# Nine pairs of z and gate tiles by seven block products, ahead of the state-space stage and through DRAM

## The chip, the cores and the metric

One core of a Trainium2 chip runs the whole decoder layer in a single launch. Its engines run side by side and meet at semaphores: TensorE (PE in the profile; its weight loads are PEld), VectorE (DVE), ScalarE (ACT) and GpSimd (POOL). SyncE (SP) and, for some tiles, ACT issue the DMAs. The metric is the device time of one execution in microseconds, the median of three runs.

## The reference, cut to what matters

The input is 1024 tokens of 1024 channels in float32. The first step multiplies them by one wide matrix; its columns are split into z, the state-space input xbc, dt, q, k, v and the gates:

```python
proj = jnp.einsum('bsd,dc->bsc', h, w_in[l])
z, xbc, dt_raw, q, k, v, gates = jnp.split(proj, SPLIT_POINTS, axis=-1)
y_ssm = mamba2_branch(z, xbc, dt_raw, ...)      # y * silu(z), then a norm over each group
y_attn = swa_sink_attention(q, k, v, ...)       # window of 128 keys, 16 heads
g_ssm, g_attn = jnp.split(jax.nn.sigmoid(gates + b_gate[l]), 2, axis=-1)
merged = (g_ssm * jnp.einsum('bsi,id->bsd', y_ssm, w_branch_ssm[l])
          + g_attn * jnp.einsum('bsi,id->bsd', y_attn, w_branch_attn[l]))
```

After the merge come an output projection, a layer norm, a feed-forward block with short convolutions, and a second layer norm. z and the gates have 2048 columns each, so 16 tiles of 128 columns each. z is used only after the state-space result of its channels exists; the gates are used only at the merge.

## The kernel before, in words

All large products run on PE with a split of every float32 factor into a high part (a cast on ACT) and a low part (the difference, on DVE or POOL); three products of parts (high by high, high by low, low by high) replace one. `dense(i)` makes one tile of 128 columns of the first projection: it loads and splits the weights (`load_w`, L103; the low part on POOL), and issues 8 x 3 x 2 = 48 matmuls of 512 moving columns into a PSUM tile `pd` of two banks. The pool `pd` has two buffers.

The program runs in stages:

- **Start.** x arrives transposed in 8 tiles and is split into `xh`, `xl`.
- **State-space stage.** Four groups of heads, `g` = 0 to 3. Each needs a B tile, a C tile and four xs tiles (`load_b`, `load_c`, `load_xs`: a dense tile, a convolution of three DVE operations out of PSUM, a silu). In each group `prep(g, hf)` and four times `unit(g, hf, i)` run for the first half of the sequence (`hf` = 0) and then for the second (`hf` = 1). Between the pieces of the first half and behind the second `prep`, `go()` places one of the six dense tiles of the next group (the gates 0 to 5 in the last group). In the second half each `unit(g, 1, i)` is followed by `zgate(g, i)`: a dense tile of z, a tanh, a DVE product out of PSUM, and the product with y.
- **Attention stage.** Tiles of k and v, then eight pairs of heads: a dense q tile, scores (`psc`), mask, bias and softmax over ACT, DVE and POOL, transposes (`ptp`), two masked copies on DVE, products with v (`py`). Gates 6 to 15 are dense tiles as well: `GPAT` places four of them behind the first halves of the first four pairs of heads, the others follow behind the pairs, and the last (`HOLD`) is issued behind the last `py`.
- **Branch projections** (`pbr`), **output projection** (`pmix`) with the first layer norm, **feed-forward** and **down projection** (`pdn`). The feed-forward block already makes its tiles two at a time with seven products of half size in place of eight (`prod`, `pair_s`, `head`, `mid`, `tail`): four half-size sums of weights, four of activations, 7 x 12 = 84 matmuls of 512 columns for two tiles.

The program is written in this order, and a scheduler then reorders the instructions of each engine by their place in the text and by when it takes their operands to be ready. Each engine runs its list in order. PSUM and SBUF tiles come from pools with a fixed number of buffers; a pool opened in the place of a closed one waits for its last readers. The tiles `tmp` of the pool `sp` have two buffers and serve the silu of xbc, the tanh of z and the first gates.

## Time and profile before

| | |
|---|---|
| median of 3 runs | 2023.79 us (2021.73 to 2023.85) |
| profiled execution | 2022.09 us, of which the instructions span 2020.3 us |
| PE busy | 1975.2 us, 98% of the span |
| DVE busy | 1351.0 us, 67% |
| POOL, ACT busy | 788.8 us (39%), 704.1 us (35%) |
| DMA | 197.5 MB moved, 98 GB/s on average |

Matmuls overlap in the pipeline, so "busy" of PE adds up durations that lie on top of each other: one matmul of 512 columns is on record with 394 ns, but the next one starts 0.227 us after it. What PE can do in a stretch is therefore read from starts, not from mean durations.

### The profile page before, as it was taken

To read this page: it belongs to the slowest core of one execution; us is meant where nothing else is said; L and a number is where in the kernel's file an instruction comes from. 1 tells how busy PE (TensorE), PEld (TensorE's weight loads), DVE (VectorE), ACT (ScalarE), POOL (GpSimd) and SP (SyncE) were. 2 spreads that over 40 slices of the span, in tenths; PEclk is the share of its full clock that TensorE was granted. 3 is DMA by queue.
4 is the path that set the end of the run, shared out by engine and by line. 5 is a ranking of instruction groups with operands and counts; after the bars stand their busy time and mean duration, and the time that the engine had idled before them with its cause. 6 is when DMAs were issued, how large, how long until landed. Compare 5 with 4: busy or idle time off the path is not lost.

```text
span 2020.3 us, 24472 instructions
## 1 busy us (share of the span) xinstructions
PE 1975.2 (98%) x9780; PEld 1614.6 (80%) x9780; DVE 1351.0 (67%) x1669; ACT 704.1 (35%) x921; POOL 788.8 (39%) x449
## 2 busy tenths in 40 slices
PE   8999999999999999999999998989999999999997
PEld 5888888888888788888888886867788888878886
DVE  6668576776355367874355368877889988863367
ACT  3334333333233334433311234234444444432122
POOL 2233233223231244442000045349999999500023
PEclk9999999999999999999999998999999999999999
DMA  4213312222332312114333344112221221264221
GB/s 161 78 60 102 126 55 94 87 81 77 112 115 84 94 53 74 42 74 157 104 105 134 137 156 156 53 55 74 92 94 73 84 94 73 81 234 154 83 84 63
DMA packets 82578, 197.50 MB, mean 98 GB/s; under 512 B 6496, under 2 KB 33696, under 8 KB 82464
## 3 DMA queue, kind: packets, MB, share of 16 engines
q1 hardware_dynamic: 76944, 191.14, 27.0%
q10 hardware_dynamic: 5520, 4.79, 0.9%
q8 instruction: 77, 1.26, 0.2%
q14 instruction: 37, 0.30, 0.0%
HBM read 153.82 MB, written 42.09 MB: 97 GB/s over the span
## 4 chain that ended last, share of the span: by engine, by line
PE 70%; issue 14%; DVE 7%; POOL 4%; DMA 3%; ACT 1%; SPq 0%; DVEq 0%; ACTq 0%; POOLq 0%
PE pd L183 32%; PE pdn L1017 11%; PE pb L724 6%; PE pc L724 4%; PE pa L724 4%; PE pmix L822 3%; PE yd L354 2%; PE yo L346 2%; PE psc L501 1%; PE py L541 1%; PE pst L320 1%; POOL sl L101 1%; DMA raw<-in_wup 1%; PE px L311 1%; DMA bsc<-trow 1%
## 5 line engine op out<-in xcount | busy, mean ns | idle before, releaser
L183 PE MATMUL pd<-xl,whi_in 128*128 128x512 f32 x1056 | 336.0, 394 | 0.0
L183 PE MATMUL pd<-xh,wlo_in 128*128 128x512 f32 x1056 | 333.8, 393 | 0.0
L183 PE MATMUL pd<-xh,whi_in 128*128 128x512 f32 x1056 | 332.8, 394 | 0.2 <-DVE xs L128 0.2
L101 POOL TENSOR_TENSOR wlo_in<-wraw_in,whi_in 128x1024 fp32r<-128x1024 f32 x66 | 162.4, 2461 | 366.6 <-ACT whi_in L100 353.1
L183 PEld LDWEIGHTS pd<-xh,whi_in 128*128 128x128 f32 x1056 | 197.2, 188 | 44.0 <-issue 3.4
L183 PEld LDWEIGHTS pd<-xl,whi_in 128*128 128x128 f32 x1056 | 197.2, 188 | 42.8 <-issue 3.8
L183 PEld LDWEIGHTS pd<-xh,wlo_in 128*128 128x128 f32 x1056 | 197.2, 188 | 40.2 <-issue 1.5
L101 POOL TENSOR_TENSOR sl<-S,sh 128x512 fp32r<-128x512 f32 x88 | 161.3, 1844 | 3.7 <-ACT sh L100 3.7
L100 ACT CAST whi_in<-wraw_in 128x1024 fp32r<-128x1024 f32 x66 | 69.4, 1051 | 209.7 <-PE pd L183 128.1
L684 POOL TENSOR_TENSOR ba<-ba,bs 128x1024 f32<-128x1024 f32 x7 | 18.8, 2694 | 259.3 <-DVE ba L683 259.3
L660 PE MATMUL pbr<-yl,whi_br 128*128 128x512 f32 x384 | 117.8, 389 | 0.0
L660 PE MATMUL pbr<-yh,wlo_br 128*128 128x512 f32 x384 | 117.4, 389 | 0.0
L660 PE MATMUL pbr<-yh,whi_br 128*128 128x512 f32 x384 | 116.7, 389 | 0.0
L1017 PE MATMUL pdn<-dh,ah 128*128 128x512 f32 x352 | 110.1, 390 | 0.6 <-ACT ah L100 0.6
L1017 PE MATMUL pdn<-dh,al 128*128 128x512 f32 x352 | 109.8, 390 | 0.3 <-DVE al L101 0.3
L1017 PE MATMUL pdn<-dl,ah 128*128 128x512 f32 x352 | 109.7, 389 | 0.0
L128 DVE SCALAR_TENSOR_TENSOR cs<-cg,colt,cs 128x1023 f32<-128x1023 f32 (+1 forms) x44 | 101.1, 2298 | 5.1 <-ACT cs L126 4.6
L583 POOL TENSOR_TENSOR out<-out,lnt 128x512 f32<-128x512 f32 x16 | 20.2, 1284 | 200.3 <-ACT out L582 200.3
L100 ACT CAST sh<-S 128x512 fp32r<-128x512 f32 x88 | 53.9, 621 | 105.2 <-POOL S L759 83.5
L128 DVE SCALAR_TENSOR_TENSOR cs<-cv,colt,cs 128x1023 f32<-128x1023 f32 (+1 forms) x44 | 85.4, 1940 | 2.0 <-ACT cs L126 2.0
L660 PEld LDWEIGHTS pbr<-yh,whi_br 128*128 128x128 f32 x384 | 72.1, 188 | 15.0
L660 PEld LDWEIGHTS pbr<-yh,wlo_br 128*128 128x128 f32 x384 | 72.1, 188 | 15.0
(305 smaller groups left out, 4321.9 us busy)
## 6 DMA issues: line engine op xcount, KB each, us to landing
wraw_in<-in_win SPq DMA_DIRECT2D x66, 512.0 KB, 3.5
m<-acd SPq DMA_DIRECT2D x32, 512.0 KB, 4.5
yraw<-ysc SPq DMA_DIRECT2D x24, 512.0 KB, 4.7
wraw_br<-in_wbr SPq DMA_DIRECT2D x24, 512.0 KB, 3.5
uraw<-in_wup SPq DMA_DIRECT2D x22, 512.0 KB, 3.5
raw<-in_wup SPq DMA_DIRECT2D x22, 512.0 KB, 4.2
asc<-cs SPq DMA_DIRECT2D x22, 512.0 KB, 2.6
draw<-in_wdn SPq DMA_DIRECT2D x22, 512.0 KB, 3.5
```

The lines of the kernel that those rows point to most:

```text
L100: A.copy(hi, raw)
L101: (eng or V).tensor_tensor(lo, raw, f(hi), ALU.subtract)
L128: V.scalar_tensor_tensor(h[:, s:], p[:, :T - s], col(c0 + taps - 1 - s), h[:, s:], ALU.mult, ALU.add)
L183: PE.matmul(p[:, q * 512:(q + 1) * 512], w[:, k * P:(k + 1) * P], x[:, q * 512:(q + 1) * 512], start=k == 0 and n == 0, stop=k == KT - 1 a ...
L311: PE.transpose(px[:, i * P:(i + 1) * P], txs[g, i][:, c * P:(c + 1) * P], ident)
L320: PE.matmul(pst, bn[:, j * P:(j + 1) * P], xdd, start=True, stop=True)
L346: PE.matmul(yo[:, j * P:(j + 1) * P], sts[j][:, i * P:(i + 1) * P], tcc[g][:, c * P:(c + 1) * P], start=True, stop=True)
L354: PE.matmul(yd[hh * 64:hh * 64 + 64, j * P:(j + 1) * P], xdts[j][:, i * P + hh * 64:i * P + hh * 64 + 64], m[:, hh, j * P:(j + 1) * P], st ...
L660: PE.matmul(p[:, q * 512:(q + 1) * 512], w[:, o:o + P], x[:, q * 512:(q + 1) * 512], start=k == 0 and n == 0, stop=k == 3 and n == 2)
L724: PE.matmul(p, a[w][:, k * P:(k + 1) * P], bop[b][x][:, k, :], start=onto is None and k == 0 and n == 0, stop=k == 3 and n == 2, skip_grou ...
L822: PE.matmul(p[q], x[tq][:, k, ts_], w[:, q * 512:(q + 1) * 512], start=k == 0 and n == 0, stop=k == KT - 1 and n == 2)
L1017: PE.matmul(p[q], x[:, j], w[:, q * 512:(q + 1) * 512], start=j == 0 and n == 0, stop=j == nf - 1 and n == 2)
```

## The change

Eighteen dense tiles leave their places: twelve of z (i = 0, 1, 2 of each group) and the gates 8 to 13. They are made in nine pairs, in a stage of their own between the start and the state-space stage, each pair by seven half-size products: 7 x 12 = 84 matmuls in place of 96. For it four sums of x are made while x arrives (on DVE, then split), and four sums of weights for each pair (on DVE, for the first pair on POOL). The results, with the tanh applied, are written to DRAM; `zgate` reads z back into a `tmp` tile, and the merge reads the gates from DRAM as it did. The gates 6 and 7 are made as ordinary dense tiles while x arrives, before the B and C tiles. Only z tiles i = 3 stay dense in the state-space stage, and only the gates 14 and 15 stay in the attention stage; the list behind `GPAT` runs out after the second pair of heads, and no gate is left for the place behind the last `py`.

```diff
+GATES = list(range(G3, 16))
+SZ = [4 * g + i for g in range(4) for i in range(3)]
+SG = GATES[2:8]
...
+        XO = [0, 4, 1, 5, 2, 6, 3, 7]
...
+            if n % 2:
+
+                p_, q_ = rawk[k - 4], raw
+                lo_, hi_ = slice(0, 512), slice(512, 1024)
+                V.tensor_tensor(p_[:, lo_], p_[:, hi_], p_[:, lo_], ALU.subtract)
+                V.tensor_tensor(p_[:, hi_], q_[:, hi_], p_[:, hi_], ALU.subtract)
+                V.tensor_tensor(q_[:, hi_], q_[:, hi_], p_[:, lo_], ALU.subtract)
+                V.tensor_tensor(q_[:, lo_], q_[:, lo_], q_[:, hi_], ALU.subtract)
+                split(q_, tb_[0][:, k - 4], tb_[1][:, k - 4])
+                split(p_, ta[0][:, k - 4], ta[1][:, k - 4])
...
+            def out0(kind, i, r):
+
+                if kind == "z":
+                    t = oo.tile([P, T], F32, tag="zt", bufs=1, name="zt")
+                    A.activation(t, r, AF.Tanh, scale=0.5)
+                    V.scalar_tensor_tensor(r, t, 1.0, r, ALU.add, ALU.mult)
+                    nc.sync.dma_start(zsc[i], r)
+                else:
+                    A.activation(r, r, AF.Tanh, bias=col(C_GB + i), scale=0.5)
+                    nc.sync.dma_start(gsc[i], r)
...
+            for i in GATES[:2]:
+                cc[i] = dense(TG + i, XO)
...
+            def prod0(p, a, b, first):
+                for k in range(4):
+                    for n, (w, x) in enumerate(((0, 0), (0, 1), (1, 0))):
+                        PE.matmul(p, a[w][:, k * P:(k + 1) * P], bop0[b][x][k],
+                                  start=first and k == 0 and n == 0, stop=k == 3 and n == 2,
+                                  skip_group_check=not first)
...
+                E = G if j == 0 else V
+                sr = {v: so.tile([P, 512], F32, tag=f"S{v}", bufs=1, name=f"S{v}") for v in range(1, 5)}
+                E.tensor_tensor(sr[1], raw1[:, lo_], raw1[:, hi_], ALU.add)
+                E.tensor_tensor(sr[2], sr[1], raw[:, lo_], ALU.subtract)
+                E.tensor_tensor(sr[3], raw[:, lo_], raw1[:, lo_], ALU.subtract)
+                E.tensor_tensor(sr[4], raw[:, hi_], sr[2], ALU.subtract)
+                for v, src in ((2, sr[2]), (1, sr[1]), (3, sr[3]), (5, raw1[:, hi_]), (4, sr[4])):
+                    t = "a22" if v == 5 else "s"
+                    h, l = (so.tile([P, 512], F32R, tag=t + w, bufs=2 if v == 5 else 4, name=t + w) for w in "hl")
+                    split(src, h, l, E)
...
+            for j in range(len(todo)):
+                head0(j)
+                if j + 1 < len(todo):
+                    if j + 1 not in R:
+                        first0(j + 1)
+                if j:
+                    tail0(j - 1)
+                mid0(j)
+                if j + 1 < len(todo):
+                    sums0(j + 1)
+            tail0(len(todo) - 1)
...
-                pz = dense(TZ + 4 * g + i)
                 t = sp.tile([P, T], F32, tag="tmp", name="tz")
-                A.activation(t, pz, AF.Tanh, scale=0.5)
-                V.scalar_tensor_tensor(t, t, 1.0, pz, ALU.add, ALU.mult)
+                if 4 * g + i in zsc:
+                    nc.sync.dma_start(t, zsc[4 * g + i])
+                else:
+                    pz = dense(TZ + 4 * g + i)
+                    A.activation(t, pz, AF.Tanh, scale=0.5)
+                    V.scalar_tensor_tensor(t, t, 1.0, pz, ALU.add, ALU.mult)
                 V.tensor_tensor(x, x, t, ALU.mult)
...
-            gates = list(range(15, G3 - 1, -1))
+            gates = [i for i in range(15, G3 - 1, -1) if i not in GATES[:2] + SG]
...
-                    for _ in range(GPAT[2 * hp + hf]):
+                    for _ in range(GPAT[2 * hp + hf] if gates else 0):
```

The scheduler's lists show what this does to the order. The first place is PE in the second half of group 2 (units 0 to 2; `yo` and `yd` are a unit's products, `pd` the dense tiles, `xh`, `xl` the parts of x). Before:

```order
L346 MATMUL yo<-cT_1836,st_5_3190 128x128
L346 MATMUL yo<-cT_1836,st_6_3204 128x128
L354 MATMUL yd<-m,xdt 64x128 x6
L183 MATMUL pd_3499<-xl_186,whi_in_3495 128x512
L183 MATMUL pd_3499<-xh_185,wlo_in_3496 128x512 x2
L183 MATMUL pd_3499<-xh_195,whi_in_3495 128x512 x2
L183 MATMUL pd_3499<-xl_196,whi_in_3495 128x512 x2
L183 MATMUL pd_3499<-xh_195,wlo_in_3496 128x512
L346 MATMUL yo<-cT_1836,st_7_3218 128x128
```

Now, at the same units:

```order
L513 MATMUL yo<-cT_3129,st_4_3868 128x128
L513 MATMUL yo<-cT_3129,st_5_4315 128x128
L513 MATMUL yo<-cT_3129,st_6_4329 128x128
L521 MATMUL yd<-m,xdt 64x128 x6
L513 MATMUL yo<-cT_3129,st_7_4343 128x128
L513 MATMUL yo<-cT_3129,st_4_3868 128x128
L513 MATMUL yo<-cT_3129,st_5_4315 128x128
L513 MATMUL yo<-cT_3129,st_6_4329 128x128
L513 MATMUL yo<-cT_3129,st_7_4343 128x128
L521 MATMUL yd<-m,xdt 64x128 x10
```

The dense tile that stood between the units' products is gone; in the list of the change, 46 rows in a row, from the `yd` of unit 2 of the first half to the `yo` of the last unit of the second, hold no matmul of a dense tile.

The second place is PE at the end of the attention stage. Before, the last pairs of heads:

```order
L183 MATMUL pd_7220<-xl_206,whi_in_7216 128x512
L541 MATMUL py<-pcur,vn 64x128
L183 MATMUL pd_7220<-xl_206,whi_in_7216 128x512
L526 MATMUL ptp<-idt,s_6928 128x128 x4
L183 MATMUL pd_7220<-xh_205,wlo_in_7217 128x512 x2
L183 MATMUL pd_7220<-xh_215,whi_in_7216 128x512 x2
L183 MATMUL pd_7220<-xl_216,whi_in_7216 128x512 x2
L183 MATMUL pd_7220<-xh_215,wlo_in_7217 128x512 x2
L541 MATMUL py<-pcur,vn 64x128
```

Now:

```order
L711 MATMUL py<-pprv,vn 64x128 x2
L696 MATMUL ptp<-idt,s_7476 128x128 x4
L711 MATMUL py<-pcur,vn 64x128
L696 MATMUL ptp<-idt,s_7513 128x128 x4
L711 MATMUL py<-pcur,vn 64x128 x3
L711 MATMUL py<-pprv,vn 64x128 x2
```

From the last matmul of the last q tile to the first `pbr` the list of the change holds 96 `psc`, 64 `ptp` and 135 `py`, and no dense tile; from the first `psc` to there it holds 403 dense matmuls, where the list before has 783.

The third place is SP's list in the second half of group 1, where the reads of z (`tz`) are new, ahead of loads that stood there already (`m` for a unit, `wraw_in` for a dense tile):

```order
L531 DMA tz<-zsc_118 128x1024
L500 DMA m<-acd 128x2x512
L531 DMA tz<-zsc_119 128x1024
L111 DMA wraw_in_4139<-in_win 128x1024
L500 DMA m<-acd 128x2x512 x2
L111 DMA wraw_in_4228<-in_win 128x1024
```

A `tz` row waits for one of the two `tmp` buffers, and the rows behind it wait with it.

## Rows read from the trace of the kernel before

**Rows 1.** The page, part 1: busy time of each engine, share, instructions.

```profile
PE 1975.2 (98%) x9780; PEld 1614.6 (80%) x9780; DVE 1351.0 (67%) x1669; ACT 704.1 (35%) x921; POOL 788.8 (39%) x449
```

**Rows 2.** The chain in order of time: start us, length us, what, count.

```profile
86.92 10.91 PE pd L183 x48
...
1506.55 2.72 PE pc L724 x12
...
1525.59 2.72 PE pc L724 x12
```

**Rows 3.** Windows: length, busy us by engine (count), PEclk granted, DMA, GB/s.

```profile
346.50:487.20 140.70, 140.70 (x761) 114.61 (x760) 100.09 (x118) 50.44 (x57) 43.42 (x24) 1.00 0.23 82
...
689.40:942.80 253.40, 252.79 (x1600) 208.35 (x1600) 176.38 (x352) 99.20 (x199) 104.95 (x80) 1.00 0.19 66
...
1470.00:1650.00 180.00, 180.00 (x795) 148.90 (x794) 164.19 (x115) 80.42 (x105) 168.31 (x85) 1.00 0.23 85
```

**Rows 4.** Windows: attention up to the first pbr, and a later stretch.

```profile
689.40:953.70 264.30, 263.69 (x1647) 217.37 (x1648) 181.21 (x356) 102.79 (x204) 104.95 (x80) 1.00 0.22 77
1200.00:1250.00 50.00, 42.16 (x169) 33.44 (x168) 41.34 (x44) 20.68 (x26) 28.14 (x11) 0.90 0.52 186
```

**Rows 5.** DVE groups, 346.5 to 487.2 us: busy us, mean ns | idle before.

```profile
L343 DVE TENSOR_TENSOR m<-m,cbm 128x1024 f32<-128x1024 f32 x8 | 11.2, 1406 | 0.1
L340 DVE TENSOR_TENSOR m<-m,acn 128x1024 f32<-128x1024 f32 x8 | 10.6, 1322 | 0.5 <-ACT ee L337 0.5
L350 DVE SCALAR_TENSOR_TENSOR ee<-xs,colt,ee 128x512 f32<-128x512 f32 x8 | 8.1, 1014 | 0.0
L366 DVE TENSOR_TENSOR xs<-xs,tz 128x1024 f32<-128x1024 f32 x5 | 6.7, 1346 | 0.1
...
L349 DVE TENSOR_TENSOR ee<-yo,ee 128x512 f32<-128x512 f32 x8 | 5.5, 685 | 2.9 <-PE yo L346 2.9
...
L128 DVE SCALAR_TENSOR_TENSOR xs<-pd,colt,xs 128x1022 f32<-128x1022 f32 x4 | 5.1, 1276 | 0.1
L365 DVE SCALAR_TENSOR_TENSOR tz<-tz,pd 128x1024 f32<-128x1024 f32 x4 | 4.9, 1218 | 2.5 <-ACT tz L364 2.5
```

**Rows 6.** DVE groups of the attention stage, 689.4 to 942.8 us.

```profile
L513 DVE TENSOR_TENSOR s<-s,bias 128x512 f32<-128x512 f32 x32 | 23.7, 742 | 0.3
L530 DVE TENSOR_TENSOR pcur<-ptp,cstt 128x512 f32<-128x512 f32 x32 | 21.9, 686 | 21.1 <-PE ptp L526 20.7
...
L520 DVE TENSOR_REDUCE mx<-s 128x4 f32<-128x512 f32 x32 | 21.9, 683 | 38.7 <-ACT s L518 38.5
...
L511 DVE COPY_PREDICATED s<-cstt,psc 128x256 f32<-128x256 int32 x48 | 20.2, 440 | 4.0 <-ACT s L510 3.9
...
L486 DVE SCALAR_TENSOR_TENSOR qs<-pd,qs 64x1024 fp32r<-64x1024 f32 x15 | 18.3, 1222 | 7.5 <-ACT qs L485 7.3
```

**Rows 7.** Timeline at the end of attention: start us, us, what.

```profile
942.83 0.59 ACT L544 COPY yat<-py 128x512 f32<-128x512 f32 x1 [0.29 <-PE py L541]
...
943.31 2.95 ACT L100 CAST yh<-yraw 128x1024 fp32r<-128x1024 f32 x3
...
944.39 3.50 DVE L101 TENSOR_TENSOR yl<-yraw,yh 128x1024 fp32r<-128x1024 f32 x3 [1.56 <-ACT yh L100]
```

**Rows 8.** Groups of the whole span: splits, and products of the feed-forward block.

```profile
L101 DVE TENSOR_TENSOR xl<-xraw,xh 128x1024 fp32r<-128x1024 f32 x8 | 9.6, 1224 | 9.7 <-ACT xh L100 9.7
...
L101 POOL TENSOR_TENSOR wlo_in<-wraw_in,whi_in 128x1024 fp32r<-128x1024 f32 x66 | 162.4, 2461 | 366.6 <-ACT whi_in L100 353.1 <-PE pd L183 12.2 <-issue 1.1
...
L100 ACT CAST whi_in<-wraw_in 128x1024 fp32r<-128x1024 f32 x66 | 69.4, 1051 | 209.7 <-PE pd L183 128.1 <-issue 62.6 <-DMA bsc<-trow 10.6
...
L932 DVE TENSOR_TENSOR cv<-p,pb 128x512 f32<-128x512 f32 x21 | 14.4, 686 | 36.8 <-PE pb L724 36.7
```

**Rows 9.** The start: timeline, then the window up to 31 us.

```profile
24.26 0.64 PE L163 MATMUL pdt<-xraw,wdr 128*32 128x256 f32 x8
...
0.00:31.00 31.00, 23.57 (x129) 14.23 (x130) 15.34 (x24) 12.45 (x14) 4.96 (x6) 1.00 0.59 226
```

More of the change, by code (lines that the diff above doesn't have):

```diff
@@ L93, in hybrid @@
     gsc = [dram.tile([P, T], F32, name=f"gsc{i}") for i in range(16)]
+    zsc = {i: dram.tile([P, T], F32, name=f"zsc{i}") for i in SZ}
     def col(i):
@@ L136, in hybrid @@
         xr_ = ExitStack()
-        xraw = xr_.enter_context(tc.tile_pool(reuse_waits="tile", name="xraw", bufs=4, side="right"))
-        pd = ph1.enter_context(tc.tile_pool(reuse_waits="tile", name="pd", bufs=2, space=bass.MemoryType.PSUM))
         pmx = {}
@@ L145, in hybrid @@
         mgt = cstt[:, K_GT:K_GT + P]
+        udt = cp1.tile([P, 256], F32, name="udt")
+        cp1.tile([P, 96], F32, name="cpad")
+        ps0 = ExitStack()
+        pdp = ps0.enter_context(tc.tile_pool(reuse_waits="tile", name="pdp", bufs=1, space=bass.MemoryType.PSUM))
+        pdt = pdp.tile([P, 512], F32, name="pdt")
+        pap = ps0.enter_context(tc.tile_pool(reuse_waits="tile", name="pap", bufs=3, space=bass.MemoryType.PSUM))
+        pd_ = ExitStack()
+        pd = pd_.enter_context(tc.tile_pool(reuse_waits="tile", name="pd0", bufs=2, space=bass.MemoryType.PSUM))
+        tt0 = ExitStack()
+        ttp = tt0.enter_context(tc.tile_pool(reuse_waits="tile", name="tt0", bufs=1, side="right"))
+        ta = [ttp.tile([P, 4, T], F32R, name=f"ta{v}") for v in "hl"]
+        tb_ = [ttp.tile([P, 4, T], F32R, name=f"tb{v}") for v in "hl"]
+        xraw = xr_.enter_context(tc.tile_pool(reuse_waits="tile", name="xraw", bufs=6, side="right"))
         wdr = xraw.tile([P, 256], F32, bufs=1, name="wdr")
         nc.sync.dma_start(wdr, wdt)
-        pre = {TB: load_w(win[TB], f"in{TB}", G)}
-        xh, xl = [], []
-        pdt = pd.tile([P, T], F32, tag="pd", name="pdt")
-        for k in range(KT):
-            raw = xraw.tile([P, 1024], F32, tag="xraw", name=f"xraw{k}")
-            (nc.scalar if k % 2 else nc.sync).dma_start(raw, xT[k * P:(k + 1) * P, :])
+        pre = {TG + GATES[0]: load_w(win[TG + GATES[0]], "in_a", G)}
+        xh, xl = [None] * KT, [None] * KT
+        XO = [0, 4, 1, 5, 2, 6, 3, 7]
+        rawk = {}
+        for n, k in enumerate(XO):
+            raw = rawk[k] = xraw.tile([P, 1024], F32, tag="xraw", name=f"xraw{k}")
+            (nc.scalar if n % 2 else nc.sync).dma_start(raw, xT[k * P:(k + 1) * P, :])
             h = xp.tile([P, T], F32R, name=f"xh{k}")
@@ L174, in hybrid, with dense @@
         V.tensor_scalar(colt[:, C_GB:C_GB + 16], colt[:, C_GB:C_GB + 16], 0.5, None, ALU.mult)
-        def dense(i):
+        A.copy(udt, pdt[:, :256])
+        def dense(i, order=range(KT)):
             hi, lo = pre.pop(i) if i in pre else load_w(win[i], f"in{i}", G)
             p = pd.tile([P, T], F32, tag="pd", name=f"pd{i}")
-            for k in range(KT):
+            for m, k in enumerate(order):
                 n = 0
@@ L190, in hybrid @@
+        ps0.close()
+        tt0.close()
+        pd = ph1.enter_context(tc.tile_pool(reuse_waits="tile", name="pd", bufs=2, space=bass.MemoryType.PSUM))
         with ExitStack() as ssm:
@@ L209, in hybrid @@
             u, e, s, q_ = tq("u"), tq("e"), tq("s"), tq("q_")
-            A.activation(u, pdt[:, :256], AF.Identity, bias=dts[:, 0:1])
+            A.activation(u, udt, AF.Identity, bias=dts[:, 0:1])
             V.scalar_tensor_tensor(e, u, -1.0, u, ALU.mult, ALU.min)
```

96 lines of the change are left out of this document (89 added, 7 removed).

## The prediction

> **What bounds the kernel now.** I read the page's engine line first. PE is busy 98% of the span, DVE 67% [rows 1], so work taken from PE is time, as long as nothing else takes its place. What a matmul is worth is read from the chain: 48 matmuls of a dense tile fill 10.91 us, 0.2273 us each, and a round of the feed-forward block, which already makes two tiles with 84 matmuls, starts 19.04 us after the one before (1506.55 to 1525.59), 0.2267 each [rows 2]. Then the windows by stage. One period of the state-space stage (group to group) is 140.7 us with PE without a gap and DVE busy 100.1; the attention stage is 253.4 us with DVE busy 176.4; the feed-forward rounds run PE without a gap beside a DVE that is busy 164.2 of 180, or 91.2% [rows 3]. So the two stages from which the change takes PE work have DVE at 71% and 70% now, and the question is what it will be there.
>
> **What PE saves.** Nine pairs, 12 matmuls less each: 108 x 0.2273 = 24.5 us, if PE stays the bound everywhere. The sum is made against the profiled execution's 2022.09 us (span 2020.3 and 1.8 around it); the median of the three runs is 1.7 us above it.
>
> **The new stage.** Its rounds have the form of the feed-forward rounds, so 19.04 us each. DVE does in a round: the low part of one weight tile (1.22), four half-size sums and five half-size low parts (nine at 0.61, half of the 1.22 of a full one, to 0.686), five sums out of PSUM at 0.686, and for z two full products at 1.22 [rows 5, 8]: 1.2 + 5.8 + 3.4 + 2.4 = 12.9 us of 19.0. It hides. ACT has 5 half casts, 1 full cast (1.05, rows 8), two half copies and two tanh, under 8 us.
>
> **The start.** DVE gets 16 half-size sums and 8 full low parts more while x arrives, some 20 us beside the 9.6 us of `xl` [rows 8]. The last x tile reaches PE at 24.3 us now, and by 31 us PE has done 129 matmuls, 64 of them the small `pdt`, so 65 of dense tiles [rows 9]. With two gate tiles in hand PE has twice the work for each x tile; the last `xl` stands behind some 20 us of DVE work that begins near 8 us, so about 30 us, and both tiles end near 36 us. Before, 22 more matmuls would have been done by then, 87 of 96: the change is 9 ahead, 2 us. Against it: the first pair's weight parts need the buffers that the gate tiles hold, so a cast (1.05) and a low part on POOL (2.46, rows 8) come after them, some 3.5 us, 1 more for the second pair, and 1 to 2 behind the first pair's sums on POOL. Net +4 us; bounds 0 (all hidden) and 12 (the sums and splits on POOL at 2.46 each, five in a row).
>
> **The state-space stage.** A period loses three dense tiles: PE 140.7 - 3 x 10.91 = 108.0 us, of which 76.4 are seven dense tiles and 31.6 the small matmuls. DVE loses three products out of PSUM at 1.22: 100.1 - 3.7 = 96.4 us, 89% of PE's. But it isn't even over the period. In the first half stand five dense tiles, in the second only two (the sixth fill and one z), where there were five. PE in the second half: 2 x 10.91 + 15.8 = 37.6 us. DVE in the second half, from [rows 5]: a unit is 1.32 + 1.41 + 1.01 and three of 0.685 = 5.80, four of them 23.2; `prep` has one mask, four scalings and three sums at 0.685, 5.5; z has four products at 1.35, three sums of squares and one product at 1.22, 10.3; the fill's convolution and silu, 3 x 1.28 + 1.3 = 5.1, of which I count half. Sum 41.6 us. A DVE that sets the pace ran at 91.2% in the fullest stretch on record [rows 3]: 41.6/0.912 = 45.6 us, 8.0 over PE. Three groups 24; in the fourth the fills are gates without convolution, 39.0/0.912 - 37.6 = 5. Together +29 us. The order agrees: in group 2, PE's list has the whole second `prep` and three units without a dense tile between them. Bounds: 0, if DVE works ahead across the halves (96.4 is under 108.0); and with DVE at the 83% (41.3 of 50) of the stretch in which PE waits most [rows 4], and the whole convolution: 44.1/0.827 - 37.6 = 15.7 for three groups and 9.6 for the fourth, +57.
>
> The reads of z cost a wait only if they come late: SP's list has an `m` load and a weight tile behind a `tz` that waits for a `tmp` buffer; both are asked for ahead of need, and their lateness lies within these bounds.
>
> **The attention stage.** From the first score matmul to the first `pbr` it takes 264.3 us [rows 4]. The lists hold 783 dense matmuls in it before and 403 now: PE alone would take 264.3 - 380 x 0.2273 = 177.9 us. DVE's work stays: 176.4, and one q split of 1.22 more [rows 3, 6]. It is uneven again. Behind the last q tile stand 96 of 256 `psc`, 64 of 128 `ptp`, 135 of 240 `py`; up to the last `py` stand 735 of the 783, so the small matmuls of the stage take 253.4 - 735 x 0.2273 = 86.3 us; by the three shares (0.38, 0.50, 0.56) PE has about 0.47 of them there, 40 us, and 138 before. DVE has there 24 of 64 masked copies, 21 of 64 reductions, 9 of 32 bias sums and 12 of 48 predicated copies: by [rows 6] (each of the two pairs of groups taken at its one row) 16.4 + 14.4 + 6.7 + 5.1 = 42.6 of these groups' 131.3 us, 32.4%. Of the 158.1 us that are left without the q splits this is 51.3 us; 126.3 stand before. At 91.2%: 138.5 and 56.2 us, 194.7 in sum. At the end the gate that PE worked on while `yh` and `yl` were made is gone: copy 0.59, cast near 1, low part 1.2 [rows 7], partly behind the high products, 3 us. 197.7 - 177.9 = +20, and 2 for matmuls slowed by the clock (below): +22 us. Bounds: with DVE without a pause, 138 + 51.3 + 2 - 177.9 = +13; at 83% and 6 us at the end, 152.7 + 62.0 + 6 - 177.9 = +43.
>
> **Sum.** 2022.1 - 24.5 + 4 + 29 + 22 = 2052.6, on the median's level 2054 us.
>
> **The clock, row and rule.** Where PE has pauses, the granted clock falls: 0.90 of full in 1200 to 1250 us, with PE busy 42 of 50 us, and 1.00 in the stages of the sum, where PE has none [rows 3, 4]. The Trainium skill, "TensorE: Matmul & The Clock Gate", section "A second HAM failure mode: psum-queue depth-cycling", says that a PE that idles briefly between groups of matmuls swings between its half and its full clock. By the row such stretches cost some 2 us, as in the sum; by the rule the end of the attention stage would run at 1.2 GHz throughout, which is the second rival. The rule speaks against the change, and the trace shows only a mild form of it.
>
> **The rivals.**
> 1. DVE does not set the pace (the other side: faster). Its queue works ahead of PE across the halves of a group, because 96.4 is under 108.0, and the state-space stage costs 0; attention costs 13, the start 1. 2023.8 - 24.5 + 14 = 2013 us. For it: PE has no gap now beside uneven DVE work, and DVE is at 91% in the feed-forward block without a loss [rows 3]. Against it: there each round has the same work, here PE's list has a stretch without dense tiles, and only two `pd` buffers let PE run ahead. It decides from the point where DVE's 41.6 us of a second half fit into 37.6 plus what it did ahead. Chance 0.14.
> 2. The clock falls in the thin stretches. The 40 us of small matmuls at the end of attention become 80 where DVE takes 56: 24 more, 2078 us; more, if the second halves follow. For it the 0.90 above; against it that the pauses are short and DVE-paced. Chance 0.16.
> 3. The new stage's rounds don't run at 19.04: sums of weights and splits for the next pair stand on DVE among this pair's sums, and single buffers of the four sums and of the second weight tile hold the next load. At 21 us a round, +18: 2072 us. For it: in the feed-forward block the splits are on POOL. Against it: 12.9 of 19 us. Chance 0.10.
> 4. The reads of z block SP: behind a late `tz` the weight tile of the next dense tile comes late, 3 to 5 us for each of 9 reads in the last three groups: +36, 2090 us. Chance 0.05.
>
> The forecast itself, both stages paced by DVE and PE at full clock, has 0.55 and its own range 2030 to 2078. A change under 0.2%, 4 us, can't be told from none here. Faster than 2020: most of rival 1, 0.12; within 4 us 0.05; slower 0.83. The range from 2020 to 2092 leaves out rival 1 and the sum of several high ends (2022 - 24.5 + 12 + 57 + 43 = 2110 and more).
>
> **What would show it.** In the profile after: `pd` at 10.9 and the new products at 19.0 us a round (else rival 3); idle time before `pd` matmuls in second halves of groups, ended by DVE, at 5 to 16 us a group (0: rival 1); the attention stage at 190 to 205 us with PE busy near 90% and DVE near 90%, its last 55 us without `pd`; a granted clock near 1.0 there (0.5 to 0.7: rival 2). Wrong throughout it would be if PE has no gaps between 200 us and the first `pbr`: then the 24.5 us stay.

## The result and the profile after

The changed kernel takes 2119.0 us (median of four runs, 2117.1 to 2120.7) against 2023.8 us before: 1.0475 times as long, 95% interval 1.0459 to 1.0491, 95.2 us more. The direction was forecast, the size was not: 2054 us was predicted, with a range up to 2092.

First the engine line of the page after, as [rows 1] of before:

```profile
PE 1987.3 (94%) x9672; PEld 1620.2 (77%) x9672; DVE 1444.0 (68%) x1817; ACT 742.3 (35%) x984; POOL 762.9 (36%) x442
```

PE has the 108 matmuls less, and 128 us of the span in which it does nothing, where before it had 45. (Busy time counts matmuls that lie on top of each other once: the first row of [rows 3] has PE busy for 140.70 of 140.70 us. So what is missing to the span is idle time.) Next, one kind of matmul at the same place of two successive rounds of the new stage (timeline: start, length):

```profile
117.92 0.39 PE L249 MATMUL pc<-tah,sh 128*128 128x512 f32 x1
...
136.96 0.39 PE L249 MATMUL pc<-tah,sh 128*128 128x512 f32 x1
```

136.96 - 117.92 = 19.04 us, the very length of the feed-forward rounds [rows 2]. That the seven products pay in full, a run below shows (e4). Now the windows, columns as in [rows 3]: the new stage, then the first and the second part of the groups 1, 2 and 3 (cut where PE stops being busy without a pause), then attention up to the last q tile and from there to the first `pbr`.

```profile
38.00:218.00 180.00, 177.39 (x778) 145.42 (x777) 100.80 (x138) 68.83 (x93) 20.27 (x13) 1.00 0.30 109
...
417.60:490.00 72.40, 72.40 (x399) 59.13 (x398) 51.93 (x65) 21.52 (x24) 22.99 (x13) 1.00 0.25 88
490.00:555.90 65.90, 52.82 (x277) 41.94 (x276) 53.91 (x57) 27.10 (x31) 17.02 (x9) 0.90 0.29 101
555.90:622.00 66.10, 66.10 (x372) 54.14 (x371) 42.10 (x57) 18.99 (x22) 22.17 (x13) 1.00 0.22 76
622.00:674.50 52.50, 32.14 (x180) 24.27 (x178) 39.56 (x46) 21.10 (x25) 10.71 (x8) 0.80 0.34 120
674.50:755.00 80.50, 80.50 (x438) 65.71 (x437) 38.02 (x54) 19.82 (x24) 25.86 (x17) 1.00 0.32 111
755.00:798.40 43.40, 29.66 (x170) 23.34 (x169) 27.09 (x32) 12.78 (x15) 5.10 (x4) 0.84 0.23 86
...
826.90:965.00 138.10, 136.58 (x839) 112.80 (x837) 103.68 (x205) 53.97 (x116) 56.88 (x44) 1.00 0.19 64
965.00:1044.50 79.50, 56.56 (x431) 45.78 (x430) 65.84 (x148) 29.86 (x72) 30.28 (x27) 0.79 0.09 34
```

Each of these groups runs in two regimes. In its first part PE has no pause and DVE is idle for a quarter or more; in the second PE pauses, and DVE is busy for 82, 75 and 62% of the time, not 91%. PE's waits between the first `pc` and the first `psc` (257.6 to 826.9 us; total, times, longest) are few and long:

```profile
PE yd L521 <- DVE m L510: 32.1, 4, 10.2
PE pst L487 <- POOL xdd L485: 18.8, 5, 5.0
PE pd L210 <- DVE k L631: 4.6, 1, 4.6
```

Before, the whole stage had one wait (61 to 689 us), and 1.8 us more right ahead of the first `psc`:

```profile
PE pd L183 <- DVE xs L128: 0.2, 1, 0.2
```

The second kind, in the second preparation of group 2 (timeline; in brackets the idle time of the engine before it, and what ended it):

```profile
625.03 0.68 DVE L480 TENSOR_TENSOR xdt<-px,dtn 128x512 f32<-128x512 f32 x1
...
625.79 1.95 POOL L485 TENSOR_TENSOR xdd<-xdt,ddec 128x512 f32<-128x512 f32 x1 [3.56 <-DVE xdt L480]
...
627.80 2.07 PE L487 MATMUL pst<-xdd,bn 128*128 128x512 f32 x2 [5.03 <-POOL xdd L485]
...
629.67 1.06 PE L478 MATMUL px<-idt,xs 128*128 128x128 f32 x4
...
630.76 0.69 DVE L480 TENSOR_TENSOR xdt<-px,dtn 128x512 f32<-128x512 f32 x1 [0.17 <-PE px L478]
...
631.67 2.02 POOL L485 TENSOR_TENSOR xdd<-xdt,ddec 128x512 f32<-128x512 f32 x1
...
633.75 2.07 PE L487 MATMUL pst<-xdd,bn 128*128 128x512 f32 x2 [3.03 <-POOL xdd L485]
```

PE's list has the transposes `px` of the next chunk behind the `pst` of this one. So each chunk goes through PE, DVE, POOL and PE in turn, 5 to 6 us a step, and nobody works ahead. Before, 30 dense matmuls (6.8 us) or more stood in front of each such `pst`, and PE waited at none. The first kind, a little later:

```profile
650.75 1.22 DVE L507 TENSOR_TENSOR m<-m,acn 128x1024 f32<-128x1024 f32 x1
651.89 0.75 DVE L517 SCALAR_TENSOR_TENSOR ee<-xs,colt,ee 128x512 f32<-128x512 f32 x1
652.55 1.22 DVE L542 TENSOR_TENSOR ss<-ss,tz 128x1024 f32<-128x1024 f32 x1
653.69 0.69 DVE L508 TENSOR_SCALAR m<-m 128x1024 f32<-128x1024 f32 x1
654.29 1.22 DVE L510 TENSOR_TENSOR m<-m,cbm 128x1024 f32<-128x1024 f32 x1
655.42 1.22 DVE L535 SCALAR_TENSOR_TENSOR tz<-tz,pd 128x1024 f32<-128x1024 f32 x1
655.66 1.98 PE L521 MATMUL yd<-m,xdt 128*64 128x128 f32 x16 [10.17 <-DVE m L510]
```

Here DVE works without a pause, on the units 2 and 3 and on z, and PE waits for it. The two phases differ: from 627.8 to 638.8 us DVE is busy for 6.1 of 11.0 us, from 640.2 to 658.0 us for 16.7 of 17.8.

In the attention stage (826.9 to 1044.5 us) PE's waits come to 22.9 us, 2.4 before. The three longest groups:

```profile
PE py L711 <- DVE pcur L700: 11.1, 11, 2.0
PE psc L671 <- DVE s L678: 6.4, 4, 2.9
PE py L711 <- ACT s L680: 3.0, 1, 3.0
```

A ledger by stage: a stage's length less its matmuls, each at the spacing that its kind has in the trace of before (0.2273 us for 512 columns), is what the stage loses. Before, 20.5 us were lost from the first `pc` to the first `psc`, and 16.3 in attention.

| | predicted | measured |
|---|---|---|
| 108 matmuls less | -24.5 | -24.5 |
| start, up to the first `pc` | +4 | +3.5 |
| state-space stage | +29 | 93.1 - 20.5 = +72.6 |
| attention | +22 | 56.0 - 16.3 = +39.7 |
| behind attention | 0 | +4.2 |
| sum | +30.5 | +95.5 (the spans differ by 95.0) |

### The profile page after: what moved, and what is told of

Same layout as the page of the kernel before. It is cut to its first block, busy times and chain, and to the rows that moved or that the text cites. A ratio compares the mean times of both kernels' runs of the same rounds, so it can differ in the third digit from the quotient of the medians.

```text
span 2115.3 us, 24624 instructions
## 1 busy us (share of the span) xinstructions
PE 1987.3 (94%) x9672; PEld 1620.2 (77%) x9672; DVE 1444.0 (68%) x1817; ACT 742.3 (35%) x984; POOL 762.9 (36%) x442
## 4 chain that ended last, share of the span: by engine, by line
PE 47%; DVE 9%; POOL 3%; DMA 2%; issue 2%; ACT 1%; SPq 0%; DVEq 0%; POOLq 0%; ACTq 0%
PE pdn L1187 11%; PE pbr L830 10%; PE pb L894 7%; PE pc L894 5%; PE pmix L992 4%; PE pa L894 4%; PE pd L210 3%; PE py L711 1%; POOL sl L107 1%; DVE hl L107 1%; DVE s L683 1%; POOL ulo L107 1%; PE psc L671 1%; DMA bsc<-trow 1%; DVE mx L685 1%
## 5 line engine op out<-in xcount | busy, mean ns | idle before, releaser
L107 POOL TENSOR_TENSOR wlo_in<-wraw_in,whi_in 128x1024 fp32r<-128x1024 f32 x46 | 118.1, 2567 | 464.7 <-ACT whi_in L106 448.2
L210 PE MATMUL pd<-xh,whi_in 128*128 128x512 f32 x736 | 237.0, 400 | 4.6 <-DVE k L631 4.6
L210 PE MATMUL pd<-xh,wlo_in 128*128 128x512 f32 x736 | 233.5, 395 | 0.0
L210 PE MATMUL pd<-xl,whi_in 128*128 128x512 f32 x736 | 233.5, 396 | 0.0
L210 PEld LDWEIGHTS pd<-xh,whi_in 128*128 128x128 f32 x736 | 138.9, 191 | 32.9 <-DVE k L631 4.7
L210 PEld LDWEIGHTS pd<-xl,whi_in 128*128 128x128 f32 x736 | 139.5, 191 | 28.9 <-issue 0.3
L210 PEld LDWEIGHTS pd<-xh,wlo_in 128*128 128x128 f32 x736 | 138.2, 189 | 29.4 <-issue 1.6
L106 ACT CAST sh<-S 128x512 fp32r<-128x512 f32 x124 | 75.9, 621 | 163.4 <-POOL S L929 73.6
L106 ACT CAST whi_in<-wraw_in 128x1024 fp32r<-128x1024 f32 x46 | 48.2, 1049 | 110.0 <-PE pd L210 81.4
L830 PEld LDWEIGHTS pbr<-yl,whi_br 128*128 128x128 f32 x384 | 72.1, 188 | 15.0
```

The costliest lines, as they stand in the source:

```text
L106: A.copy(hi, raw)
L107: (eng or V).tensor_tensor(lo, raw, f(hi), ALU.subtract)
L210: PE.matmul(p[:, q * 512:(q + 1) * 512], w[:, k * P:(k + 1) * P], x[:, q * 512:(q + 1) * 512], start=m == 0 and n == 0, stop=m == KT - 1 a ...
L830: PE.matmul(p[:, q * 512:(q + 1) * 512], w[:, o:o + P], x[:, q * 512:(q + 1) * 512], start=k == 0 and n == 0, stop=k == 3 and n == 2)
```

## The experiments

All start from the changed kernel unless told otherwise. Times are medians; in brackets the ratio to the kernel before with its interval. "Loss" is that of the ledger.

**Which part costs what.** `SZ = []` leaves z where it was, `SG = []` the gates 8 to 15:

```diff
-SZ = [4 * g + i for g in range(4) for i in range(3)]
+SZ = []                       # e1_gates_only
-SG = GATES[2:8]
+SG = []                       # e2_z_only
```

> Only the gates 6 to 13 leave their places (three pairs, 36 matmuls less, 8.2 us); all z tiles stay dense in the state-space stage. Theory A (a stage loses where PE's list has no dense tile beside a chain of waits, and each stage loses by itself): the state-space periods are 140.6 us again, the attention stage keeps its +40 us over what its matmuls need and the branch projections their +4, the new stage some +8: 2023.8 - 8.2 + 8 + 44 = 2068, within 2060 to 2076. Rival (the attention stage lost only because the state-space stage handed its lists over late, or the loss is spread over all stages): attention within +20, 2030 to 2050.

Measured: 2056.1 us (1.0160, 1.0145 to 1.0175). The rows are a state-space period, and the attention stage:

```profile
462.10:602.90 140.80, 140.80 (x762) 114.61 (x760) 97.43 (x114) 50.34 (x57) 42.31 (x24) 1.00 0.25 87
772.30:983.80 211.50, 188.71 (x1263) 154.93 (x1263) 169.30 (x354) 85.11 (x188) 86.39 (x72) 0.94 0.13 50
```

The period is that of before; the state-space loss is 19.1 us, attention's 50.8, 34.5 more than before and not 40, so the time is 4 us below theory A's range. The losses belong to their stages.

> Only the twelve z tiles are made in pairs (six pairs, 72 matmuls less, 16.4 us), and the gates 6 and 7 stay at the front; the gates 8 to 15 are dense in the attention stage. Theory A: the state-space stage keeps its loss of about 70 us (23 up to the end of group 0, of which 8 in the new stage, then 30, 11 and 14), the attention stage loses 0 to 5: 2023.8 - 16.4 + 78 + 3 = 2088, within 2080 to 2096. Rival (as in the prediction, DVE's amount of work sets the pace, 8 us a group): 2023.8 - 16.4 + 8 + 29 = 2044.

Measured: 2102.8 us (1.0387, 1.0371 to 1.0402). State-space loss 93.9 us, as in the full change; attention loses 31.3, 15 more than before, with only two of its ten gates gone. More than either side said, on theory A's side.

**Place or product?** Each pair as two plain dense tiles, in the new stage and through DRAM:

```diff
-            for j in range(len(todo)):
-                head0(j)
...
+            for kind, i0, i1 in todo:
+                for i in (i0, i1):
+                    p_ = dense((TZ if kind == "z" else TG) + i)
```

> The same eighteen tiles in the same new stage and through DRAM, but as plain dense tiles of 96 matmuls a pair; no sums of x or of weights. If the place alone costs and the seven products pay in full: later than the changed kernel by 108 x 0.2273 = 24.5 us less the 4 to 8 us that the start of the seven products costs, so 2135 to 2144. If the seven products pay nothing (their stage paced by DVE): 2115 to 2122.

Measured: 2144.9 us (1.0597, 1.0581 to 1.0613), 25.8 later than the changed kernel and 0.9 beyond the range of the first side; state-space loss 97.6, attention 56.1. The place costs 121 us (2144.9 against 2023.8), the seven products give their 24.5 back (25.8 by these two runs).

**Does any dense tile do as cover?** The fill tiles of a group are held behind small matmuls:

```diff
-                go()
+                go("pc" if g else ("pst", 0))
+                go(("pst", 1 if g else 2))
...
-                    go()
+                    if i == 1:
+                        go(("yd", 0))
```

(the other three stand behind `pc`, the second `pst` and the first unit's `yd` of the second half)

> Same work on every engine as the changed kernel; only PE's order differs: the six fill tiles of a group are held back until certain small matmuls, so that dense matmuls stand in the second halves of the groups too (16 to 28 behind most of the score and state matmuls there, where the changed kernel has 0 to 10). Theory A (uncovered chains, not DVE's amount of work): periods of 108 to 114 us, most of the 55 us of long gaps gone, 2060 to 2080. Rival B (DVE's amount of work, or buffers of the unit chain, set the pace of the second halves): DVE's work is the same, 119 to 138 us a period as now, 2105 to 2120. Rival C (the loss is the clock's): as A, if the gaps go; the granted clock tells how much.

Measured: 2143.6 us (1.0593, 1.0574 to 1.0611), 25 slower, against every theory. The waits:

```profile
PE pr L549 <- DVE ss L542: 41.9, 3, 14.1
PE pst L487 <- POOL xdd L485: 17.1, 4, 5.1
PE prt L557 <- DVE rt L124: 9.6, 3, 3.2
```

The `yd` waits are down to 4.0 us, but the fills bring their convolutions (three of 1.27 us on DVE) into the units, and the ends of the first three groups wait for DVE. The fourth group, whose fills are gates without a convolution, is the exception: PE waits 3.2 us in it (704 to 858 us), and 18.3 in the changed kernel (684 to 827 us). So a tile whose result DVE must read at once is no free cover here; a tile that DVE need not read was, in this one group.

**Cover without DVE work.** 48 dummy matmuls behind each second preparation:

```diff
                 prep(g, 1)
                 go()
+                pw = pd.tile([P, T], F32, tag="pd", name="pw")
+                for n in range(24):
+                    for q in range(2):
+                        PE.matmul(pw[:, q * 512:(q + 1) * 512], xh[n % KT][:, :P], ...)
```

> The changed kernel with one more tile's worth of dense matmuls in each group's second half, 48 of 512 columns on operands that are there already, whose result nobody reads: 4 x 10.9 = 43.6 us of PE work, none for DVE, ACT, POOL or the queues. If PE only waits in the second halves (theories D and L), most of it goes into the pauses: 2119 to 2135. If the half clock in the thin stretches costs much (rival C), the busier PE gains some of it back: below 2117. If PE is the bound after all: 2155 to 2163.

Measured: 2136.8 us (1.0560, 1.0542 to 1.0577), just beyond the edge of what the waits alone would give: 17.8 us for 43.6 us of matmuls. In group 0 the dummies stand in the second half; in the others the scheduler drew them into the first, and in group 1 the real tiles that they displaced stand in the second. The periods 1, 2 and 3:

```profile
421.00:564.30 143.30, 141.02 (x759) 114.20 (x760) 111.06 (x126) 52.95 (x60) 43.24 (x23) 1.00 0.28 92
564.30:689.30 125.00, 106.16 (x572) 84.19 (x571) 85.88 (x102) 38.17 (x46) 30.98 (x19) 0.89 0.26 89
689.30:822.00 132.70, 120.89 (x662) 98.34 (x661) 65.61 (x86) 33.95 (x41) 31.57 (x20) 0.95 0.27 96
```

Group 1 has 19.8 us more matmul work than in the changed kernel and takes 143.3 in place of 138.2 us, at full clock; PE's waits in it fall from 13.1 to 2.3 us. Groups 2 and 3, whose second halves stay bare, lose 31.6 and 18.9 us. The loss is pauses that dense matmuls used to fill, and the half clock that goes with them: the granted clock of group 1 is 1.00 here and 0.95 in the changed kernel.

**Buffers, DVE's work, the chain.** Four `ee` and four `m` buffers; the z product and the sum of squares on POOL; no z product at all; `xdd` on DVE:

```diff
-                ee = sp.tile([P, 512], F32, tag="ee", name="ee")
+                ee = sp.tile([P, 512], F32, tag="ee", bufs=4, name="ee")     # e5 (and m: bufs=4)
-                V.tensor_tensor(x, x, t, ALU.mult)
+                E = G if 4 * g + i in zsc else V                              # e6
+                E.tensor_tensor(x, x, t, ALU.mult)                            # e6 (and ss)
-                        G.tensor_tensor(v3(xdd), v3(xdt), bch(ddec, g, c), ALU.mult)
+                        V.tensor_tensor(v3(xdd), v3(xdt), bch(ddec, g, c), ALU.mult)   # e7
```

> The changed kernel with four buffers in place of two for ee and four in place of three for m, so that the exponentials and the m reads of units 2 and 3 need not wait for units 0 and 1. Theory D (in the unit stretch of a second half DVE works back to back, and its amount of work there sets the time): no change, 2115 to 2123, and the waits of yd for DVE stay at 8 to 10 us a group. Rival B (too few buffers: the unit chain starts late): most of the 32 us of yd waits go, 2088 to 2100.

Measured: 2101.2 us (1.0383, 1.0367 to 1.0400), loss 79.2. Theory D fails, but the rival isn't the whole either: the `yd` waits give way to waits of dense tiles for a `pd` buffer that DVE has still to read:

```profile
PE pd L210 <- DVE tz L535: 25.8, 4, 11.7
PE pst L487 <- POOL xdd L485: 9.6, 4, 3.5
PE pd L210 <- DVE xs L134: 8.3, 4, 5.5
```

> The changed kernel with the product of y and z and the sum of squares of the twelve moved tiles on POOL in place of DVE: three products and two sums of 1.22 us less on DVE in each group, 24 us in all; POOL needs about 2.4 us for each. Theory D: the yd waits shrink by up to 6 us a group: 2095 to 2108. Rival B (buffers, or the length of the chain, which POOL makes longer): 2115 to 2130.

Measured: 2131.4 us (1.0532, 1.0515 to 1.0550), 12 slower, just beyond rival B's range and for a reason that it didn't name (last section).

> The changed kernel without the product of y and z for the twelve moved tiles, without their part in the sum of squares (the first tile of a group aside) and without their reads from DRAM: this work is left out. DVE loses 3 products and 2 sums of 1.22 us in each group, 24.4 us in the stage; PE loses nothing. Theory D (DVE sets the time of the unit stretches, by work and by order): 20 to 35 us less, 2084 to 2099. Rival (latency of the chains alone): 2112 to 2120. It also bounds what the reads can cost.

Measured: 2107.2 us (1.0413, 1.0396 to 1.0429), 12 less for 24 us of DVE work, between the two. Group 2 lost nothing more than before, group 3 lost 46.0: PE's list came out otherwise, with the dense tiles spent earlier, so the run doesn't measure DVE's work alone.

> The changed kernel with the second scaling of the preparation (xdd) on DVE in place of POOL, so that a step of the chain from the transposes (px) over two scalings to the state product (pst) is shorter by POOL's 2 us less DVE's 0.69; DVE gets 28 x 0.69 = 19 us more in the stage. Theory L (the waits of pst in the second halves are the length of that chain, 18.8 us in the trace of the changed kernel): they shrink to 8 to 11, 2105 to 2115. Rival D (DVE's amount of work sets the time of a second half): 2124 to 2138.

Measured: 2121.3 us (1.0485, 1.0469 to 1.0500), no difference, between the two: the `pst` waits fell to 13.8 us, the `yd` waits rose to 39.1.

**How few tiles are free?** `SZ = [0, 4, 8, 12]`, `SG = []`:

> Only the four z tiles i = 0 are made in pairs (two pairs, 24 matmuls less, 5.5 us), the gates 6 and 7 at the front, the other gates in the attention stage as in the kernel with only z moved, whose attention stage takes 258.4 us where the matmuls left would need 242.5, 16 more. Theory A (there is a loss only where the chains stand without a dense tile): four dense tiles stay in each second half and PE's list has about 30 dense matmuls before each state matmul, so the state-space stage loses 0 to 8: 2023.8 - 5.5 + 3 + 16 + 4 = 2041, within 2036 to 2048. Rival (each tile that is taken costs the same, 70 us by three): 2023.8 - 5.5 + 3 + 16 + 23 = 2060.

Measured: 2065.3 us (1.0206, 1.0191 to 1.0221), on the rival's side: state-space loss 42.8, 22.3 more than before for four tiles. Attention was as expected. The list had its 30 matmuls before each `pst` and no `pst` wait was left, but `pd` waited for DVE (11.2 and 5.5 us in sum). Theory A in this form falls: cover of the preparation is not enough.

**The tile without a convolution beside the chain.** On e5, the z tile that stays dense is made behind the second preparation, in a tile of its own:

```diff
                 prep(g, 1)
+                z3(g)            # dense, tanh and product into its own tile
                 go()
```

> The kernel with more buffers (ee, m), and in each group the one z tile that is still dense is made directly behind the second preparation, into a tile of its own, in place of behind the last unit. Same work on every engine. PE's list now has 23 to 47 dense matmuls before nearly every pst of a second half, where the changed kernel has 0 to 24. Theory A (the loss is the pauses of the chains without cover; a tile without convolution covers without adding DVE work in the way): the state-space stage loses 25 to 45 us in place of 93 (of which the kernel before has 20): 2051 to 2071. Rival (too little dense work is left in all, wherever it stands): 2090 to 2103, as with the buffers alone.

Measured: 2099.7 us (1.0370, 1.0356 to 1.0385), loss 75.1: the rival's. The `pst` waits are down to 3.1 us; in their place stand

```profile
PE pr L553 <- DVE ss L540: 10.8, 2, 9.6
PE pd L210 <- ACT gt L569: 9.7, 1, 9.7
PE pd L210 <- DVE cT L134: 6.8, 1, 6.8
```

> As e13_z3_early, but with the gates 8 to 15 dense in the attention stage (only z in pairs). If the losses of the two stages are independent: 8.2 us more matmuls, and the attention stage loses 31 in place of 56 us: 16 us below the time of e13_z3_early, 2035 to 2055.

Measured: 2081.9 us (1.0287, 1.0270 to 1.0303); state-space loss 77.5, attention 31.3. It misses its range as e13 did, but 17.8 us below e13 it shows the stages independent.

> As e13_z3_early, but all ten gates stay where the kernel before has them; two z tiles (0 and 4) are the plain dense tiles of the start, the other ten are five pairs, 60 matmuls less, 13.6 us. Attention loses nothing, the start 5, the state-space stage what e13_z3_early shows (5 to 25 more than before): 2020 to 2040. Faster than the kernel before only if the state-space stage loses under 9 us.

Measured: 2077.4 us (1.0258, 1.0244 to 1.0272); attention's loss 18.5, near that of before; state-space loss 77.8. Five pairs give 13.6 us and cost 57 there, far over the 9 that were allowed. No version beat the kernel before.

**Order or clock?** Dummies inside the pauses, 8 or 24 at eight places (e14), and one at each of the same places (e18):

```diff
                         pst = ps("pst")
+                        if hf and (g, j) in ((1, 1), (2, 0), (2, 1), (2, 2), (3, 2)):
+                            filler(pst, 8, last)         # e18: 1
...
                 yd = ps("yd")
+                if hf and g and i == 2:
+                    filler(yd, 24, S["yo"])              # e18: 1
```

> The changed kernel with dummy matmuls (8 of 512 columns before each of the five state products that have none before them, 24 before yd of unit 2 in the groups 1 to 3; 112 in all, 25 us at full clock), written into the PSUM tile that the true product then overwrites: PE works where it waited, the chains stay as they are. Theory C (the half clock in the thin stretches costs a good part of the 73 us): 2105 to 2112. Rival (the chains set the time, the clock beside them costs next to nothing): 2116 to 2126.

Measured: 2099.8 us (1.0371, 1.0357 to 1.0385), 19 less, more than theory C said.

> As e14_filled_pauses, at the same eight places and with the same constraints of order, but with one dummy matmul at each in place of 8 or 24. Theory C (keeping PE busy in the pauses keeps the clock up, and that is the 19 us): the gain is gone, 2112 to 2120, with half-clock stretches of about 60 us in the state-space stage as in the changed kernel. Rival (the changed order of the px, pst and yo matmuls brought it): 2097 to 2105.

Measured: 2106.2 us (1.0407, 1.0391 to 1.0422): 12.8 of the 19 us come without the work of the dummies. Why, the timeline of e18's group 2 shows (L457 is a dummy):

```profile
621.63 0.60 PE L483 MATMUL px<-idt,xs 128*128 128x128 f32 x4
622.55 0.50 PE L457 MATMUL pst<-xh 128*128 128x512 f32 x1 [0.32 <-DVE xs L533]
623.15 0.66 PE L483 MATMUL px<-idt,xs 128*128 128x128 f32 x4
623.58 0.50 PE L457 MATMUL pst<-xh 128*128 128x512 f32 x1
623.91 0.60 PE L483 MATMUL px<-idt,xs 128*128 128x128 f32 x4
625.78 1.12 PE L494 MATMUL pst<-xdd,bn 128*128 128x512 f32 x2 [1.27 <-POOL xdd L490]
```

Three chunks are transposed before the first `pst`, where the changed kernel transposes one, waits 5.03 us, and goes on. The stage's `pst` waits fall from 18.8 to 6.3 us, its `yd` waits stay (31.7). That is the order of a few small matmuls, the rival. It isn't the order alone: with fewer pauses the granted clock of the stage is 0.96 in e18, 0.95 in the changed kernel. With the dummies' work come 6.4 us more, by the ledger 3 in the state-space stage and 5 in attention, whose list came out otherwise, less 2 at the start. The granted clock of the state-space stage is 0.98 with it, so what it gains from 0.96 to 0.98 is at most these 6.4 us, as far as the dummies themselves delay nothing.

**Attention.** The two gates that it keeps are held to the last pairs of heads (e9); the bias sum is left out (e12); dummies stand before `py` at its end (e17):

```diff
+            for at in ((5, 0), (6, 0)):                    # e9, in place of GPAT
+                with tc.issue_after(pyref[at]):
+                    gate(gates.pop(), gtp, "gt")
-                        V.tensor_tensor(s3, s3, bias[...], ALU.add)        # e12
+                    if hp >= 5:                            # e17: 8 matmuls into py
```

> The changed kernel with the two gates that the attention stage still has (14 and 15) held back to the last three pairs of heads; their matmuls stand among the scores, transposes and py there, where the changed kernel has none. Theory A for attention (the end of the stage has no dense tile beside its chains): 22 us of matmuls go into the pauses of the last 75 us, the front of the stage stays covered by the q tiles: 10 to 18 us less, 2101 to 2109. Rival (the stage is paced by DVE throughout, whatever the order): 2115 to 2123.

Measured: 2116.4 us (1.0458, 1.0442 to 1.0473): attention loses 54.7 in place of 56.0. The rival holds: from 1002 to 1044 us PE is busy for 36.7 in place of 30.6 us, but the pauses moved to the middle of the stage.

> The changed kernel without the sum of scores and position bias in the attention stage: this sum is left out, 32 operations of 0.73 us on DVE, 23.4 us; PE's work is the same. Theory D for attention (DVE's work, 169.5 us of the stage's 217.6, sets its time, since the kernel with the gates held back gained nothing): 15 to 24 us less, 2095 to 2104. Rival (the latency of the softmax chain over ACT and POOL): 0 to 6 us less, 2113 to 2119.

Measured: 2105.3 us (1.0411, 1.0395 to 1.0426); attention loses 14.7 us less: just short of theory D's range, far from the rival's. PE's waits in the stage fall from 22.9 to 16.4 us, and its granted clock rises from 0.92 to 0.97, so a part of the gain came as faster matmuls.

> The changed kernel with eight dummy matmuls of 512 columns before the first py matmul of each half of the last three pairs of heads, written into the PSUM tile that the true products overwrite; 48 in all, 10.9 us at full clock. Theory C for attention (half clock costs there too, some 13 us in the trace of the changed kernel): 2105 to 2115. Rival (DVE sets the time of the end of the stage, the clock of PE is hidden by it): 2117 to 2128.

Measured: 2121.8 us (1.0484, 1.0466 to 1.0502), no difference, while the clock of the end rose from 0.79 to 0.85 in a stretch of the same length with DVE as busy:

```profile
967.00:1046.50 79.50, 61.51 (x481) 50.66 (x479) 67.28 (x149) 29.70 (x71) 30.03 (x27) 0.85 0.09 34
```

## Why the prediction was right in direction and wrong in size

**What PE saves: right.** 108 x 0.2273; the round of 19.04 us is that of the trace, and e4 is 25.8 us slower without it. Rival 3 falls.

**The start: right.** +3.5 where +4 stood; two PE waits for POOL's low part, as named.

**The state-space stage: the place was right, the wait was another, and the term was mis-sized by 44 us.** The failed step is "41.6/0.912 = 45.6 us". DVE's amount was right on average (53.9, 39.6 and 27.1 us in the second parts of the groups 1, 2 and 3, where 41.6 stood and 39.0 for the last), the pace was not: 82, 75 and 62%, in 65.9, 52.5 and 43.4 us. The 91.2% came from feed-forward rounds, in which dense work of one pair lies beside DVE's work for another [rows 3]. In the second half of a group nothing does: while the preparation goes step by step through PE, DVE and POOL, DVE is idle for almost half of the time, and then its work comes in one burst, at 94% in group 2. The forecast had the burst's work and put the waiting of the first phase at nothing. Nor do the waits stand where it expected them, before `pd` matmuls: there is one of 4.6 us there. From the timeline, DVE's longest stretch with no pause over 0.6 us is 22.4 us before and 38.2 after. Of PE's waits 18.8 us fall into the first of these phases, 32.1 into the second. My upper bound, at 83%, was +57: taken from one stretch of another stage [rows 4], it was still too quick.

Of the 72.6 us, 55.5 are the three waits listed above; the rest lies in matmuls that start further apart, many of them at half clock. No single cause was found to own the 55.5. More buffers took 14 us off the stage, earlier `px` 12 (e18), no z product 10, the better cover 18 together with the buffers, and in each other waits stayed or came: the losses of e5, e10, e13, e16 and e18 are 79, 83, 75, 78 and 81. What is shown is that a group whose second half is covered loses next to nothing more than before (4.8 and 7.3 us in the groups 0 and 1 of e11, about 5 each before), that tiles with much DVE work in the same place don't help (e3, where in the one group with gates in their place PE hardly waits), and that even one z tile of a group is worth half of its 10.9 us as cover (e8: 22.3 us for four). How the rest divides between DVE's burst and the order of PE's list stays open.

**Attention: the length of the first part was right by luck, the end mis-sized.** Up to the last q tile 138.5 us were predicted, from 126.3 us of DVE work at 91.2%, and 138.1 measured. But PE was busy for 136.6 of them and DVE for 103.7, so DVE didn't set this part: PE's own work, 138 us in the prediction, happened to be as long. DVE was 22.6 us behind its forecast when the last q tile ran. For the end 51.3 us of DVE work were expected at 91.2%, 56.2 us and 3 more; there were 65.8 us at 83%, 79.5 us. The failed step is the share of 32.4%: it was counted in PE's list, as if DVE kept step with it, and 39% of DVE's 169.5 us were left. (The four groups behind the share add up to 131.5 us by [rows 6], not 131.3; the share stays 32.4%.) That DVE's work sets the stage, e12 shows best, with 14.7 us less for 23.4 us of work left out; e9 and e17, in which PE's order and its clock changed and the time did not, agree.

**The clock: a small price, not fully separated.** The granted clock, which is an average over stretches at 1.2 and at 2.4 GHz, was 0.79 at the end of attention and 0.80 in the second part of group 2. For attention I had 2 us, for the state-space stage nothing. Single rows show what half clock does: two `pst` take 2.07 us after a pause and 1.12 in e18, four `px` 1.06 and 0.60. How much of the kernel's time this is, the runs only bound: from 0.96 to 0.98 in the state-space stage 6.4 us (e14 against e18), from 0.79 to 0.85 at the end of attention nothing, beside 48 dummies that take PE time of their own (e17). Rival 2, with half clock throughout the end of attention and 24 us for it, is not borne out: the clock was 0.79, neither the 0.5 to 0.7 of its sign nor near 1.0. But of attention's 39.7 us the waits are only 20.5 more than before, and the other 19 lie in matmuls that start further apart. That these are hidden behind DVE's work is argued from e12 and e17, and not shown for all of them. The Trainium skill, "TensorE: Matmul & The Clock Gate", section "A second HAM failure mode: psum-queue depth-cycling", says that a PE that idles often between groups of matmuls swings between its clocks. The trace agrees here, with 0.79 and 0.80, more than I had allowed; half clock throughout, as I had read it, neither the section says nor the trace shows.

**Rival 1 falls** with the waits; **rival 4** as well: among PE's long waits none leads to a read of z, and e10, without these reads and with less DVE work, gained only 12 us.

## What to carry to other kernels

An engine that is busy 98% of the span may owe it to filler work beside chains of waits; count, stage by stage, what stands in its list between a chain's steps before taking that work away, and price the removed filler at the pauses it covered (here some 120 us lost for 24.5 saved). A busy share that another engine reaches in an evenly filled stretch is no pace for a stretch in which it first waits and then has everything at once. And in these runs a tile was free cover only where the late engine didn't have to read it soon.

## What the runs showed of the hardware that was not expected

POOL and DVE slow each other. In the changed kernel POOL's second scaling (`xdd`) takes 1.04 us at the median of its 28 times, but 1.95 and 2.02 us in the two steps shown above, beside which DVE is at work; so a part of that chain's length is this. With the z products on POOL (e6), each takes 2904 ns there on average (1.22 us on DVE):

```profile
L537 POOL TENSOR_TENSOR xs<-xs,tz 128x1024 f32<-128x1024 f32 x12 | 34.7, 2904 | 43.1 <-PE yd L521 37.5 <-DVE xs L524 5.6
```

Some operations that stayed on DVE grew. First the changed kernel's clamp of m, from 260 to 810 us (busy us, mean ns | idle before):

```profile
L508 DVE TENSOR_SCALAR m<-m 128x1024 f32<-128x1024 f32 x30 | 23.4, 779 | 0.1
```

and the same in e6:

```profile
L508 DVE TENSOR_SCALAR m<-m 128x1024 f32<-128x1024 f32 x31 | 41.1, 1326 | 0.1
```

So 24 us taken from DVE came back as slower DVE work: over the whole span DVE is busy for 1450.2 us in e6 and 1444.0 in the changed kernel. The kernel lost 12. The Trainium skill, "SBUF — State Buffer", section "SBUF: two separate sides", says that DVE and GpSimd share a pair of ports that one holds for a whole instruction; these rows agree.
